# Turning the output projection's rows and the V values on VectorE in 32x32 squares instead of on TensorE

## The chip, the core and the metric

The kernel runs on one core of one Trainium2 chip. The metric is the time of one execution on the device in microseconds; of several runs the median counts. A core has five engines, each with an instruction stream of its own, which wait for each other by semaphores: TensorE (PE: matmuls; PEld is its weight loads), VectorE (DVE), ScalarE (ACT), GpSimd (POOL) and SyncE (SP), which here only issues DMA transfers. ScalarE issues some transfers too. An engine takes its stream in the order in which it is written, so an instruction that waits holds up those behind it.

## The reference: what is computed

One step of a two-layer streaming encoder, 2048 prompt rows and 32 sample rows of width 1024, in float32. Cut to the parts that the change touches:

```python
def delta_layer(x, ...):                       # layer A
    ...
    o, s_new = gated_delta_rule(q, k, v, g, beta, s0)
    o = o * lax.rsqrt(jnp.mean(o * o, -1, keepdims=True) + RMS_EPS) * norm_w * jax.nn.silu(z)
    out = o.reshape(b, l, A_VW) @ w_out        # output projection of layer A
    return layer_norm(DN_ALPHA * x + out, ln_g, ln_b), new_buf, s_new

def shared_kv(h, w_kv, pos):                   # h is layer A's result
    kv = h @ w_kv
    k = rope_partial(kv[..., :B_KVW]..., pos)
    v = kv[..., B_KVW:]...
    return k, v

def swa_layer(x, k, v, ...):                   # layer B
    proj = x @ w_in                            # queries and gates
    ...                                        # banded or cached attention on k, v
    return layer_norm(DN_ALPHA * x + (o * jax.nn.silu(z)) @ w_out, ln_g, ln_b)
```

`layer_norm` takes mean and variance of a row, and gives (x - mean) * rsqrt(var + eps) * g + b.

## The kernel before, in words

Float32 products are made of three matmuls each of high and low parts (`_hi`, `_lo`). The program has five stages: the projections and convolutions of layer A (to about 700 us), the delta rule (to about 1120 us), the output projection O1 of layer A (from 1080 to 1333 us, its first tiles woven into the delta rule's end), the projections P2 of layer B (from about 1310 to 1700 us, its first steps woven into O1's end) and the attention with the second output projection.

**O1** (classes `OutNorm` and `O1`) goes over 17 tiles of 128 rows, the last of 32. For each tile `g` (the gated result, with the channel on the partition) is loaded and split: ScalarE casts the high part `g_hi` (L1168), VectorE subtracts the low part `g_lo` (L1169). `r` (rows of x) is loaded (L1161). For each of two halves of 512 columns, TensorE makes 24 matmuls (L1126 to L1128) into a PSUM bank `po`, and VectorE empties the bank into `r` (L1134) and takes statistics (L1186). Then VectorE gets mean and inverse deviation by a chain of small instructions on a column (L1188 to L515), and normalizes `r` in four instructions of 512 columns (L1203, L1205). `r` is stored as `h` (L1265, to the memory `s_h`). `turned` is a generator: eight TensorE transposes of 128x128 in two groups of four (L1232), each group copied from PSUM to `hT` by ScalarE or VectorE (L1234), then one store of 512 KB to `s_hT` (L1236), in runs of 128 tokens (512 bytes). Its two groups are interleaved late in the matmuls of the next tile. `po` has two banks; the transposes take a third and fourth, which are two `po` banks for the first tiles and the `ps` banks of P2 once that exists.

**Order.** A scheduler sets the order on the engines, except where a block fixes TensorE's order, or more engines', as written: TensorE, VectorE and ScalarE during the delta rule; TensorE and VectorE in O1's rest; all engines in P2. SP issues the loads of `g` and `r` for tiles below about 10, then ScalarE does. `r`, `g_hi` and `g_lo` have two buffers each, `g` and `hT` have one.

**P2** goes over column blocks of 416 tokens. For the two tiles that hold V, `turn` turns the 128x416 block `c` (ten calls): four TensorE transposes of 128x104 into the one bank `tp` (L1714), two ScalarE copies of 104x256 into two `o` buffers (L1718), each with a store by ScalarE's queue to `s_bv` (L1719). The `o` buffers are shared with all other work of P2 (11 of them). The weights' low part `w_lo` is made by VectorE (L1330).

Of the kernel before, what the change touches and what calls it, by code (L numbers as in the profile page):

```python
# [1140 lines left out]
class OutNorm:  # L1141
# [21 lines left out]

    def split(self, g, n):
        nc = self.nc
        ghi = self.two.tile([128, KC, 128], F32R, tag="g_hi", name="g_hi")
        glo = self.two.tile([128, KC, 128], F32R, tag="g_lo", name="g_lo")
        nc.scalar.copy(ghi[:, :, :n], g[:, :, :n])  # L1168
        nc.vector.tensor_tensor(out=low_part(ghi, glo, n), in0=g[:, :, :n], in1=ghi[:, :, :n], op=ALU.subtract)  # L1169
        return ghi, glo  # L1170

    def tile(self, parts, r, n, tail=False):
# [5 lines left out]
        for c in range(2):  # L1178
            cs = slice(c * 512, c * 512 + 512)
            ps = self.pp.tile([128, 512], F32, tag="po", name="po")  # L1180
            for k in range(KC):
                out_products(nc, ps, ghi, glo, (w[0][:, k, cs], w[1][:, k, cs]), k, n)
                if k % 2 == 1:
                    yield (4 if n <= 64 else 6) * 0.227
            add_products(nc, r, glo, ps, cs, n)
            V.bn_stats(out=st[:n, c, :], in_=r[:n, cs])  # L1186
# [7 lines left out]
        if not tail:  # L1194
            nb = self.two.tile([128, 1], F32, tag="nb", name="nb")
            V.scalar_tensor_tensor(out=nb[:n], in0=mv[:n, 0:1], scalar=-1.0, in1=rs[:n], op0=ALU.mult, op1=ALU.mult)
            nc.scalar.activation(r[:n], r[:n], AF.Identity, bias=nb[:n, 0:1], scale=rs[:n, 0:1])
            nc.gpsimd.tensor_tensor(out=r[:n], in0=r[:n], in1=tabs[0][:n], op=ALU.mult)
            nc.gpsimd.tensor_tensor(out=r[:n], in0=r[:n], in1=tabs[1][:n], op=ALU.add)
        else:  # L1200
            for c in range(2):
                cs = slice(c * 512, c * 512 + 512)
                V.scalar_tensor_tensor(out=r[:n, cs], in0=r[:n, cs], scalar=mv[:n, 0:1], in1=tabs[0][:n, cs],  # L1203
                                       op0=ALU.subtract, op1=ALU.mult)
                V.scalar_tensor_tensor(out=r[:n, cs], in0=r[:n, cs], scalar=rs[:n, 0:1], in1=tabs[1][:n, cs],  # L1205
                                       op0=ALU.mult, op1=ALU.add)
# [3 lines left out]
class O1:  # L1210
    def __init__(self, tc, es, I, O, T, G):
        self.nc, self.I, self.T, self.G = tc.nc, I, T, G
        self.on = OutNorm(tc, es, "o1", "left", I, "a", 2, T["wo"])
        self.bank = lambda: self.on.pp.tile([128, 512], F32, tag="po", name="tr")
        self.steps = 0
        self.room = lambda: self.on.one.tile([128, KC, 128], F32, tag="g", name="hT")
# [7 lines left out]
    def turned(self, h, c0, row, n):  # L1224

        nc, T = self.nc, self.T
        hT = self.room()
        for q in range(2):
            tr = self.bank()[:].rearrange("p (j t) -> p j t", j=4)
            for j in range(4):  # L1230
                k = q * 4 + j
                nc.tensor.transpose(tr[:, j, :n], h[:n, k * 128:k * 128 + 128], self.G["ident"][:n, :n])  # L1232
            copy = nc.scalar.copy if n == 128 and (q == 0 or c0 == 0) else nc.vector.tensor_copy
            copy(hT[:, q * 4:q * 4 + 4, :n], tr[:, :, :n])  # L1234
            if q == 1:
                nc.sync.dma_start(T["hT"][:, :, c0:c0 + n].rearrange("h p t -> p h t"), hT[:, :, :n])  # L1236
            yield 0.44

    def tiles(self, tiles, ready, more):


        late = iter(())
# [5 lines left out]
        for i, t in enumerate(tiles):  # L1248
# [9 lines left out]
            for j, out in enumerate(self.on.tile(got, r, t[2], True)):  # L1258
                if isinstance(out, float):
                    yield out  # L1260
                    if j == 3 and ahead is not None:
                        ahead = self.on.split(ahead, tiles[i + 1][2])
                    if j >= 6:
                        yield from itertools.islice(late, 1)
            self.nc.sync.dma_start(self.T["h"][t[1]:t[1] + t[2], :], out[:t[2]])  # L1265
            late = self.turned(out, *t)
# [4 lines left out]
        yield from late  # L1271


class P2:
# [29 lines left out]
    def open_left(self, left):  # L1304
# [4 lines left out]
        self.py = new_pool(self.tc, left, "p2_py", 1, PSUM, side="left")  # L1309
# [400 lines left out]
    def turn(self, c, half, b):  # L1710
        nc, w = self.nc, TB // 4
        tp = self.py.tile([128, 4, 128], F32, tag="tp", name="tp")
        for j in range(4):
            nc.tensor.transpose(tp[:w, j, :], c[:, j * w:j * w + w], self.ident[:, :])  # L1714
        rows = self.T["bv"][b * TB:(b + 1) * TB, half * 128:half * 128 + 128].rearrange("(j t) x -> t j x", j=4)
        for js in (slice(0, 2), slice(2, 4)):
            v = self.out()[:, 0:256].rearrange("p (j x) -> p j x", j=2)
            nc.scalar.copy(v[:w], tp[:w, js])  # L1718
            nc.scalar.dma_start(rows[:, js], v[:w])  # L1719
# [519 lines left out]
def program(tc, I, O, T, G):  # L2239
# [75 lines left out]
    o1[0].room = lambda: hp.tile([128, KC, 128], F32, tag="hT", name="hT")  # L2315
    o1[0].bank = p2[0].ps
# [216 lines left out]
```

## Time and profile before

| What | Value |
|---|---|
| Time, median of 3 runs | 2101.48 us (2099.33 to 2110.56) |
| The profiled execution: time and span | 2110.58 us; span 2108.8 us |
| Busy: PE, DVE, ACT, POOL | 97%, 70%, 47%, 43% of the span |
| Granted TensorE clock, mean | 0.989 |
| 1150 to 1250 us (O1): PE, DVE, ACT busy | 100.00, 81.24, 18.23 us of 100 |
| 1400 to 1700 us (P2): PE, DVE, ACT busy | 293.78, 232.95, 139.92 us of 300 |
| DMA packets; bytes | 292763; 360.85 MB |

How to read it: a row of the timeline has start, duration, engine, line, operation, out<-in by the program's names, and in brackets the engine's idle time before and what ended it. `SPq` and `ACTq` are transfers that these engines issue. A row of a group ends with its busy time, the mean in ns of one instruction, and the idle time before them with what ended most of it. A TensorE row with x4 is a run of four matmuls, whose times overlap.

### The profile page before, as it was taken

Reading aid. Unit: us, or ns where it says so; the run is one execution under the profiler, and the core shown is the slowest. Engines: PE = TensorE matmul, PEld = TensorE weight load, DVE = VectorE, ACT = ScalarE, POOL = GpSimd, SP = SyncE. Lnnn points to the kernel's source line nnn. Section 1 sums busy time; section 2 is a strip of 40 time slices with the busy share of each in tenths; the row PEclk is TensorE's granted clock in tenths of the full one; section 3 lists DMA queues with packets and bytes.
Section 4 is the critical chain, followed back from the end, with each engine's and each line's share of the span. In section 5 each row is a group of like instructions: output and inputs, shape, how many; then the busy total and the mean of one; then the engine's idle time right before and its main releaser. Section 6 shows DMA issues by size and latency. Waiting matters only on the chain.

```text
span 2108.8 us, 37301 instructions
## 1 busy us (share of the span) xinstructions
PE 2048.6 (97%) x13694; PEld 1875.4 (89%) x13694; DVE 1468.9 (70%) x2587; ACT 989.0 (47%) x2465; POOL 911.0 (43%) x1248
## 2 busy tenths in 40 slices
PE   7999999999999999999999999999999999999998
PEld 5999999999999999999887887889989997777775
DVE  4476666675647678888887887768877755566565
ACT  4354444446532267777762211534644445455552
POOL 0322223212222177778752112157436515566666
PEclk9999999999999999999999999999999999999999
DMA  5132333236665545455766666778776659533421
GB/s 206 33 90 88 97 110 111 82 102 226 193 185 179 182 137 179 159 169 182 271 209 227 212 213 219 254 229 296 243 240 222 226 171 317 127 101 107 114 72 66
DMA packets 292763, 360.85 MB, mean 171 GB/s; under 512 B 74260, under 2 KB 217460, under 8 KB 292564
## 3 DMA queue, kind: packets, MB, share of 16 engines
q1 hardware_dynamic: 278576, 334.29, 49.9%
q10 hardware_dynamic: 14004, 24.17, 3.6%
q8 instruction: 108, 1.77, 0.3%
q14 instruction: 75, 0.61, 0.1%
HBM read 235.54 MB, written 134.06 MB: 175 GB/s over the span
## 4 chain that ended last, share of the span: by engine, by line
PE 83%; DMA 7%; DVE 3%; POOL 3%; issue 2%; ACT 1%; SPq 0%; ACTq 0%; DVEq 0%; POOLq 0%
PE ps L79 12%; PE ps L81 11%; PE ps L80 11%; PE ot L1126 3%; PE ot L1127 3%; PE ot L1128 3%; PE S L1992 2%; PE po L1126 2%; PE ot L2025 2%; PE po L1128 2%; PE po L1127 2%; PE tr L2007 2%; PE X L1653 2%; PE X L1651 2%; PE X L1652 2%
## 5 line engine op out<-in xcount | busy, mean ns | idle before, releaser
L79 PE MATMUL ps<-act_hi,w_hi 128*128 128x416 f32 x1280 | 454.9, 355 | 0.0
L81 PE MATMUL ps<-act_hi,w_lo 128*128 128x416 f32 x1280 | 450.2, 352 | 0.0
L80 PE MATMUL ps<-act_lo,w_hi 128*128 128x416 f32 x1280 | 447.9, 350 | 0.0
L79 PEld LDWEIGHTS ps<-act_hi,w_hi 128*128 128x128 f32 x1280 | 240.3, 188 | 3.8 <-issue 0.4
L80 PEld LDWEIGHTS ps<-act_lo,w_hi 128*128 128x128 f32 x1280 | 240.6, 188 | 3.0
L81 PEld LDWEIGHTS ps<-act_hi,w_lo 128*128 128x128 f32 x1280 | 240.1, 188 | 3.3
L209 DVE SCALAR_TENSOR_TENSOR y<-R,convw,y 128x2083 f32<-128x2083 f32 x72 | 182.5, 2536 | 60.9 <-ACT y L206 44.9
L56 POOL TENSOR_TENSOR w_lo<-w_raw,w_hi 128x1024 fp32r<-128x1024 f32 x25 | 71.4, 2858 | 330.9 <-ACT w_hi L55 303.6
L729 POOL TENSOR_TENSOR tm<-L,Tt 128x60 f32<-128x60 f32 (+19 forms) x365 | 132.5, 363 | 84.8 <-issue 39.9
L1826 POOL TENSOR_TENSOR P<-e,sm 128x384 f32<-128x384 f32 (+2 forms) x128 | 102.3, 820 | 118.0 <-DVE sm L1816 111.6
L731 POOL TENSOR_TENSOR Tt<-Tt,tm 128x60 f32<-128x60 f32 (+19 forms) x365 | 139.8, 383 | 28.6
L1812 ACT ACTIVATE e<-S,nm 128x193 f32<-128x193 f32 (+2 forms) x260 | 104.6, 415 | 97.3 <-DVE nm L1807 56.5
L1330 DVE TENSOR_TENSOR w_lo<-w_raw,w_hi 128x512 fp32r<-128x512 f32 x132 | 136.7, 1053 | 18.5 <-ACT w_hi L1342 12.7
L1126 PE MATMUL po<-wo_hi,g_hi 128*128 128x512 f32 x256 | 104.9, 410 | 8.1 <-DVE r L1134 7.9
L305 ACT COPY R<-ps 128x416 f32<-128x416 f32 (+1 forms) x144 | 60.4, 442 | 109.3 <-PE ps L81 95.8
L1482 ACT ACTIVATE o<-X 128x416 f32<-128x416 f32 x80 | 41.4, 518 | 134.7 <-PE X L1653 134.6
L1126 PE MATMUL ot<-wo,g_hi 128*128 128x512 f32 x256 | 103.6, 405 | 0.0
L1128 PE MATMUL po<-wo_hi,g_lo 128*128 128x512 f32 x256 | 101.2, 396 | 0.5 <-DVE g_lo L1169 0.5
L1127 PE MATMUL po<-wo_lo,g_hi 128*128 128x512 f32 x256 | 101.1, 395 | 0.0
L1127 PE MATMUL ot<-wo,g_hi 128*128 128x512 f32 x256 | 100.8, 394 | 0.0
L1128 PE MATMUL ot<-wo,g_lo 128*128 128x512 f32 x256 | 100.8, 394 | 0.0
L1342 ACT CAST w_hi<-w_raw 128x512 fp32r<-128x512 f32 x129 | 76.8, 616 | 21.5 <-PE ps L1652 6.7
(362 smaller groups left out, 5119.4 us busy)
## 6 DMA issues: line engine op xcount, KB each, us to landing
w_raw<-in_b_w SPq DMA_DIRECT2D x60, 512.0 KB
w_raw<-in_w_in SPq DMA_DIRECT2D x40, 512.0 KB
act_raw<-s_hT SPq DMA_DIRECT2D x64, 208.0 KB
s_rows<-o SPq DMA_DIRECT2D x50, 208.0 KB
k<-s_k SPq DMA_DIRECT2D x17, 512.0 KB
E<-s_E SPq DMA_DIRECT2D x17, 512.0 KB
s_bq<-s_rows SPq DMA_DIRECT2D x40, 208.0 KB
s_bz<-o SPq DMA_DIRECT2D x40, 208.0 KB
```

The lines of the kernel that those rows point to most:

```text
L79: nc.tensor.matmul(ps, hi[:, k, :], xh[:, k, :], start=(k == 0), stop=False)
L80: nc.tensor.matmul(ps, hi[:, k, :], xl[:, k, :], start=False, stop=False)
L81: nc.tensor.matmul(ps, lo[:, k, :], xh[:, k, :], start=False, stop=(k == KC - 1))
L209: nc.vector.scalar_tensor_tensor(out=y[:], in0=R[:, j:j + W], scalar=self.convw[:, i, j:j + 1], in1=y[:], op0=ALU.mult, op1=ALU.add)
L729: P.tensor_tensor(out=tm[:n, i0 - k:, :w], in0=L[:n, i0:, j:j + 1].to_broadcast(sh), in1=Tt[:n, j:j + 1, :w].to_broadcast(sh), op=ALU.mult)
L731: P.tensor_tensor(out=Tt[:n, i0:, :w], in0=Tt[:n, i0:, :w], in1=tm[:n, i0 - k:, :w], op=ALU.subtract)
L1126: nc.tensor.matmul(ps[:n], ghi[:, k, :n], hi, start=a, stop=False)
L1127: nc.tensor.matmul(ps[:n], ghi[:, k, :n], lo, start=False, stop=False)
L1128: nc.tensor.matmul(ps[:n], glo[:, k, :n], hi, start=False, stop=z)
L1330: P.tensor_tensor(out=lo, in0=raw, in1=hi, op=ALU.subtract)
L1812: self.nc.scalar.activation(x.e[:, h, u, :x.n], x.S[:, h, u, :], AF.Exp, bias=x.nm[:, h, u:u + 1], scale=1.0, accum_out=x.sm[:, h, u:u + 1])
L1826: self.nc.gpsimd.tensor_tensor(out=x.P[:, u, :nj * 128].rearrange("r (j h k) -> r j h k", h=2, k=64), in0=x.e[:, :, u, :n].rearrange("r h ...
```

## The change

The tile's rows are turned by one VectorE instruction, `transpose`, which turns each square of 32x32 in its place. The squares are put where they belong by the store: four transfers of 32 partitions each, in runs of 32 tokens (128 bytes). `turned` is no generator any more and runs at the tile's end. The normalization becomes one small VectorE instruction (`nb`), one ScalarE Identity with scale and bias over 128x1024, and two VectorE products with the tables over 128x1024. The second half of a tile takes its bank from P2's `ps` once P2 exists, so that with it there are four banks. In P2 V is turned in the same way into one `o` buffer, and four stores by ScalarE's queue follow one step later; the bank `tp` is gone, and that pool (`py`) has two.

```diff
+    spare = None
+    def bank(self, c):
+        if c and self.spare:
+            return self.spare()
+        return self.pp.tile([128, 512], F32, tag="po", name="po")
...
-            ps = self.pp.tile([128, 512], F32, tag="po", name="po")
+            ps = self.bank(c)
...
-            for c in range(2):
-                cs = slice(c * 512, c * 512 + 512)
-                V.scalar_tensor_tensor(out=r[:n, cs], in0=r[:n, cs], scalar=mv[:n, 0:1], in1=tabs[0][:n, cs],
-                                       op0=ALU.subtract, op1=ALU.mult)
-                V.scalar_tensor_tensor(out=r[:n, cs], in0=r[:n, cs], scalar=rs[:n, 0:1], in1=tabs[1][:n, cs],
-                                       op0=ALU.mult, op1=ALU.add)
+        nb = self.two.tile([128, 1], F32, tag="nb", name="nb")
+        V.tensor_scalar(out=nb[:n], in0=mv[:n, 0:1], scalar1=rs[:n, 0:1], scalar2=-1.0, op0=ALU.mult, op1=ALU.mult)
+        nc.scalar.activation(r[:n], r[:n], AF.Identity, bias=nb[:n, 0:1], scale=rs[:n, 0:1])
+        V.tensor_tensor(out=r[:n], in0=r[:n], in1=tabs[0][:n], op=ALU.mult)
+        V.tensor_tensor(out=r[:n], in0=r[:n], in1=tabs[1][:n], op=ALU.add)
...
         hT = self.room()
-        for q in range(2):
-            tr = self.bank()[:].rearrange("p (j t) -> p j t", j=4)
-            for j in range(4):
-                k = q * 4 + j
-                nc.tensor.transpose(tr[:, j, :n], h[:n, k * 128:k * 128 + 128], self.G["ident"][:n, :n])
-            copy = nc.scalar.copy if n == 128 and (q == 0 or c0 == 0) else nc.vector.tensor_copy
-            copy(hT[:, q * 4:q * 4 + 4, :n], tr[:, :, :n])
-            if q == 1:
-                nc.sync.dma_start(T["hT"][:, :, c0:c0 + n].rearrange("h p t -> p h t"), hT[:, :, :n])
-            yield 0.44
+        self.nc.vector.transpose(hT[:n], h[:n])
+        rows = self.T["hT"].rearrange("h (c j) t -> j (h c) t", j=32)
+        for a in range(0, n, 32):
+            self.nc.sync.dma_start(rows[:, :, c0 + a:c0 + a + 32],
+                                   hT[a:a + 32].rearrange("j (c i) -> j c i", i=32))
...
-        self.py = new_pool(self.tc, left, "p2_py", 1, PSUM, side="left")
+        self.py = new_pool(self.tc, left, "p2_py", 2, PSUM, side="left")
...
     def turn(self, c, half, b):
-        nc, w = self.nc, TB // 4
-        tp = self.py.tile([128, 4, 128], F32, tag="tp", name="tp")
-        for j in range(4):
-            nc.tensor.transpose(tp[:w, j, :], c[:, j * w:j * w + w], self.ident[:, :])
-        rows = self.T["bv"][b * TB:(b + 1) * TB, half * 128:half * 128 + 128].rearrange("(j t) x -> t j x", j=4)
-        for js in (slice(0, 2), slice(2, 4)):
-            v = self.out()[:, 0:256].rearrange("p (j x) -> p j x", j=2)
-            nc.scalar.copy(v[:w], tp[:w, js])
-            nc.scalar.dma_start(rows[:, js], v[:w])
+        nc, t = self.nc, self.out()
+        nc.vector.transpose(t[:], c[:])
+        rows = self.T["bv"][b * TB:(b + 1) * TB, half * 128:half * 128 + 128]
+        rows = rows.rearrange("(b i) (a j) -> a i b j", i=32, j=32)
+
+        def store():
+            for a in range(4):
+                s = slice(32 * a, 32 * a + 32)
+                nc.scalar.dma_start(rows[a], t[s].rearrange("i (b j) -> i b j", j=32))
+
+        self.delay(store, 1)
...
-    o1[0].bank = p2[0].ps
+    o1[0].on.spare = p2[0].ps
```

Where the order on the engines moves, it is shown before and after. First VectorE in a steady tile of O1, from the end of the column chain (L515) to the second half's statistics; before:

```order
L515 TENSOR_SCALAR ln_y<-ln_t,ln_y 128x1
L1203 SCALAR_TENSOR_TENSOR r<-r,mv,ln_g 128x512
L1205 SCALAR_TENSOR_TENSOR r<-r,ln_y,ln_b 128x512
L1203 SCALAR_TENSOR_TENSOR r<-r,mv,ln_g 128x512
L1205 SCALAR_TENSOR_TENSOR r<-r,ln_y,ln_b 128x512
L1169 TENSOR_TENSOR g_lo<-g,g_hi 128x1024
L1134 SCALAR_TENSOR_TENSOR r<-r,po 128x512
L1186 BN_STATS st<-r 128x6
L1234 COPY hT<-ps 128x512
L1134 SCALAR_TENSOR_TENSOR r<-r,po 128x512
L1186 BN_STATS st<-r 128x6
```

and after:

```order
L515 TENSOR_SCALAR ln_y<-ln_t,ln_y 128x1
L1202 TENSOR_SCALAR nb<-mv,ln_y 128x1
L1204 TENSOR_TENSOR r<-r,ln_g 128x1024
L1205 TENSOR_TENSOR r<-r,ln_b 128x1024
L1226 STREAM_TRANSPOSE hT<-r 128x1024
L1176 TENSOR_TENSOR g_lo<-g,g_hi 128x1024
L1134 SCALAR_TENSOR_TENSOR r<-r,po 128x512
L1193 BN_STATS st<-r 128x6
L1134 SCALAR_TENSOR_TENSOR r<-r,ps 128x512
L1193 BN_STATS st<-r 128x6
```

The four normalizing instructions became `nb`, two products and the turn, with ScalarE's Identity between `nb` and the first product; the copy of `hT` between the two halves is gone.

Next ScalarE at the end of the delta rule (L784 to L903 are the delta rule's, `vs` is what its next matmuls read); before:

```order
L784 COPY ta<-tp 64x256 x2
L794 COPY u<-up 64x8x64 x2
L803 COPY ta<-y2p 64x256 x2
L813 ACTIVATE u<-u2p 64x4x64 x2
L863 COPY vs<-vp_11841 128x512
L884 COPY o<-op_11807 128x512
L863 COPY vs<-vp_11885 128x512
L903 ACTIVATE vn,Xo<-o 128x128 x4
```

and after:

```order
L784 COPY ta<-tp 64x256 x2
L794 COPY u<-up 64x8x64 x2
L803 COPY ta<-y2p 64x256 x2
L813 ACTIVATE u<-u2p 64x4x64 x2
L1203 ACTIVATE r<-r,nb,ln_y 128x1024
L863 COPY vs<-vp_11841 128x512
L884 COPY o<-op_11807 128x512
L863 COPY vs<-vp_11892 128x512
L903 ACTIVATE vn,Xo<-o 128x128 x4
```

The Identity of tile 0 (L1203) stands ahead of the copy of `vs`.

Last SP's transfers around the loads of `g` for tiles 2 to 4 (L1156); `w_raw` are weights of P2, and `s_g<-z` stores the delta rule's results; before:

```order
L1236 DMA s_hT<-hT 128x8x128
L1336 DMA w_raw<-in_b_w 128x1024 x4
L679 DMA z<-s_z 128x4x32
L1156 DMA g<-s_g 128x1024
L1265 DMA s_h<-r 128x1024
L1336 DMA w_raw<-in_b_w 128x1024
L932 DMA s_g<-z 128x4x32
L932 DMA s_g<-z 128x512 x2
L1161 DMA r<-in_x 128x1024
L1156 DMA g<-s_g 128x1024
L1236 DMA s_hT<-hT 128x8x128
L1265 DMA s_h<-r 128x1024
```

and after:

```order
L679 DMA z<-s_z 128x4x32
L1325 DMA w_raw<-in_b_w 128x1024 x2
L932 DMA s_g<-z 128x4x32
L1255 DMA s_h<-r 128x1024
L1229 DMA s_hT<-hT 32x32x32 x4
L1161 DMA r<-in_x 128x1024
L932 DMA s_g<-z 128x512 x2
L1156 DMA g<-s_g 128x1024 x2
L1255 DMA s_h<-r 128x1024
L1229 DMA s_hT<-hT 32x32x32 x4
L1161 DMA r<-in_x 128x1024
L1156 DMA g<-s_g 128x1024
```

Before, a load of `g` stands between the weights' loads, ahead of the second store of `h`; after, two loads of `g` stand behind that store, its four `hT` stores and the load of `r`.

More of the change, by code (lines that the diff above doesn't have):

```diff
@@ L1170, in split, with tile @@
         return ghi, glo
-    def tile(self, parts, r, n, tail=False):
+    def tile(self, parts, r, n):
         nc, V = self.nc, self.nc.vector
@@ L1213, in __init__ @@
         self.on = OutNorm(tc, es, "o1", "left", I, "a", 2, T["wo"])
-        self.bank = lambda: self.on.pp.tile([128, 512], F32, tag="po", name="tr")
         self.steps = 0
-        self.room = lambda: self.on.one.tile([128, KC, 128], F32, tag="g", name="hT")
+        self.room = lambda: self.on.one.tile([128, D], F32, tag="g", name="hT")
     def fetch(self, c0, row, n):
@@ L1257, in tiles @@
             self.on.queue = self.nc.sync if i < 9 else self.nc.scalar
-            for j, out in enumerate(self.on.tile(got, r, t[2], True)):
+            for j, out in enumerate(self.on.tile(got, r, t[2])):
                 if isinstance(out, float):
@@ L1262, in tiles @@
                         ahead = self.on.split(ahead, tiles[i + 1][2])
-                    if j >= 6:
-                        yield from itertools.islice(late, 1)
             self.nc.sync.dma_start(self.T["h"][t[1]:t[1] + t[2], :], out[:t[2]])
-            late = self.turned(out, *t)
+            self.turned(out, *t)
             got, r = ahead, following
@@ L1270, in tiles @@
         yield from more(2)
-        yield from late
 class P2:
@@ L2314, in program @@
     hp = new_pool(tc, last, "o1_hT", 1, side="right")
[L2315 to L2316 removed]
+    o1[0].on.spare = p2[0].ps
+    o1[0].room = lambda: hp.tile([128, D], F32, tag="hT", name="hT")
     later = []
```

9 lines of the change are left out of this document (removed).

## The prediction

> **What bounds the kernel now.** I read the page first, its busy shares and the chain of waits.
>
> ```profile
> PE 2048.6 (97%) x13694; PEld 1875.4 (89%) x13694; DVE 1468.9 (70%) x2587; ACT 989.0 (47%) x2465; POOL 911.0 (43%) x1248
> PE 83%; DMA 7%; DVE 3%; POOL 3%; issue 2%; ACT 1%; SPq 0%; ACTq 0%; DVEq 0%; POOLq 0%
> ```
>
> TensorE is busy for 97% of the span and holds 83% of the chain, so work taken from it shortens the kernel wherever no other engine is just behind. That must be asked of two stages: the layer A output projection (O1, 1080 to 1333 us) and the pass over the V tiles (1340 to 1700 us). Next, TensorE's own waits between 1080 and 1720 us (engine, line, waited for: total, times, longest), and who held VectorE's L1134 up.
>
> ```profile
> PE po L1126 <- DVE r L1134: 7.9, 3, 3.8
> PE ps L1653 <- DVE w_lo L1330: 4.8, 2, 3.6
> PE tp L1714 <- ACT o L1718: 3.2, 2, 3.0
> PE sp L846 <- ACT vs L863: 1.2, 1, 1.2
>   DMA r<-in_x: 5.2, 2
> ```
>
> In O1 TensorE waits three times for VectorE to empty a bank (L1134), and two of those wait in turn for a load of `r`. In the V turns it waits for ScalarE's copies. Then one tile of O1 in the timeline, TensorE and VectorE.
>
> ```profile
> 1171.92 0.39 PE L1128 MATMUL po<-wo_hi,g_lo 128*128 128x512 f32 x1
> 1172.15 0.60 PE L1232 MATMUL ps<-ident,r 128*128 128x128 f32 x4
> 1172.51 0.48 PE L1126 MATMUL po<-wo_hi,g_hi 128*128 128x512 f32 x1
> ```
>
> ```profile
> 1172.79 0.69 DVE L1234 COPY hT<-ps 128x512 f32<-128x512 f32 x1 [1.91 <-PE ps L1232]
> 1173.40 0.68 DVE L1134 SCALAR_TENSOR_TENSOR r<-r,po 128x512 f32<-128x512 f32 x1
> 1177.26 0.74 DVE L1203 SCALAR_TENSOR_TENSOR r<-r,mv,ln_g 128x512 f32<-128x512 f32 x1
> 1180.16 1.22 DVE L1169 TENSOR_TENSOR g_lo<-g,g_hi 128x1024 fp32r<-128x1024 f32 x1
> 1181.30 0.68 DVE L1134 SCALAR_TENSOR_TENSOR r<-r,po 128x512 f32<-128x512 f32 x1
> 1182.02 0.69 DVE L1186 BATCH_NORM_STATS2 st<-r 128x6 f32<-128x512 f32 x1
> 1184.62 0.69 DVE L1234 COPY hT<-ps 128x512 f32<-128x512 f32 x1 [1.91 <-PE ps L1232]
> ```
>
> The period is 1184.62 - 1172.79 = 11.83 us. VectorE is idle for only 1.91 of it, waiting for TensorE. So TensorE bounds a steady tile, and VectorE is second with 9.92 us of work.
>
> **The change, part by part.** *TensorE's transposes in O1.* A group of four occupies 1172.15 to 1172.51, 0.36 us, and the next matmul is 0.48 instead of 0.39 us: 0.44 us a group. Two groups in each of 17 tiles are 34 groups, 15.0 us. A tile needs TensorE for 11.83 - 0.88 = 10.95 us afterwards.
>
> *VectorE's work per tile.* The copy of `hT` goes (1173.40 - 1172.79 = 0.61 us), as do the four L1203/L1205 (1180.16 - 1177.26 = 2.90). What stays is 9.92 - 0.61 - 2.90 = 6.41: the L1134-to-L1203 chain 3.86, g_lo 1.14, and L1134 with its statistics 1.41. What comes instead:
>
> ```profile
> L225 DVE STREAM_TRANSPOSE R<-th 128x2080 f32<-128x2080 f32 x16 | 37.5, 2341 | 37.8 <-ACT th L224 37.8
> L717 DVE STREAM_TRANSPOSE L<-nb 128x1024 f32<-128x1024 f32 x16 | 32.3, 2019 | 1.7 <-ACT nb L708 1.7
> L841 DVE TENSOR_TENSOR k<-k,gb 128x1024 f32<-128x1024 f32 x16 | 20.1, 1257 | 12.2 <-PE ktr L818 12.2
> L1881 ACT ACTIVATE r<-r,nb,ln_y 128x1024 f32<-128x1024 f32 x15 | 18.7, 1246 | 4.5 <-DVE nb L1877 4.5
> L1877 DVE TENSOR_SCALAR nb<-mv,ln_y 128x1 f32<-128x1 f32 x15 | 3.2, 215 | 0.5
> ```
>
> The new `nb` is 0.2 us (L1877). Then VectorE waits for ScalarE's Identity over 128x1024: 1.25 us (L1881) and about 0.1 of handing over. Behind that wait stand on VectorE both products with the tables, the turn, the next tile's g_lo and the L1134 that empties TensorE's bank. Each product is 1.14 (g_lo's slot, the same shape) to 1.26 us (L841). The turn over 1024 columns is 1.15 us by L225 (2341 x 1024/2080), or 2.02 by L717, whose input is a strided broadcast. `r` and `hT` are plain rows like L225's, so I take 1.15. Sum: 6.41 + 0.2 + 1.35 + 2 x 1.14 + 1.15 = 11.4 us; high end 6.41 + 0.2 + 1.35 + 2 x 1.26 + 2.02 = 12.5. So VectorE replaces TensorE as the bound of a steady tile: 11.4 against 10.95, a gain of 0.4 of the 0.88 us.
>
> The Trainium skill, VectorE: DVE Perf Modes, section "The three transpose paths", gives VectorE 311 ns for a 128x128 bf16 transpose of 32x32 blocks. By that figure eight such squares would be an estimated 2.5 us and the tile 12.8; no run here shows bf16, and L225 is against it with 144 ns a square.
>
> *The start of O1.* The order puts tile 0's Identity ahead of ScalarE's `vs` copy, where TensorE's delta rule waits (L846 above, already 1.2 us).
>
> ```profile
> 1112.24 0.59 ACT L863 COPY vs<-vp 128x512 f32<-128x512 f32 x1 [2.59 <-PE vp L846]
> 1115.25 0.21 DVE L515 TENSOR_SCALAR ln_y<-ln_t,ln_y 128x1 f32<-128x1 f32 x1
> 1137.54 0.53 SPq L1156 DMA_DIRECT2D g<-s_g  x1
> 1144.21 1.04 ACT L1168 CAST g_hi<-g 128x1024 fp32r<-128x1024 f32 x1 [10.17 <-DMA g<-s_g]
> ```
>
> The column `ln_y` is ready at 1115.46, so `vs` starts near 1115.46 + 0.2 + 1.25 = 1116.9 instead of 1112.24; of these 4.7 us about 1.6 lie beside other TensorE work: 3.1 us. On SP the load of g for tile 3 loses more. Before, it is issued at 1137.54 and cast 6.67 us later; now it stands behind s_h of tile 1, its four hT stores and a load of `r` that waits for that s_h to land, by my walk near 1147.7. Tile 3's first matmul, at 1147.26 before, then comes near 1155. This +7.7 contains the 3.1, and the wait of 2.9 us that was there.
>
> *Tiles 3 to 15.* The first and last of the 13 L1134:
>
> ```profile
> 1161.56 0.68 DVE L1134 SCALAR_TENSOR_TENSOR r<-r,po 128x512 f32<-128x512 f32 x1
> 1310.62 0.68 DVE L1134 SCALAR_TENSOR_TENSOR r<-r,po 128x512 f32<-128x512 f32 x1
> ```
>
> Twelve periods took 149.1 us, with two waits for `r` and a slow stretch after each long TensorE wait, as here:
>
> ```profile
> 1284.47 0.47 PE L1126 MATMUL po<-wo_hi,g_hi 128*128 128x512 f32 x1 [3.85 <-DVE r L1134]
> 1285.24 0.63 PE L1126 MATMUL po<-wo_hi,g_hi 128*128 128x512 f32 x1
> 1285.67 0.63 PE L1127 MATMUL po<-wo_lo,g_hi 128*128 128x512 f32 x1
> 1288.65 0.39 PE L1128 MATMUL po<-wo_hi,g_lo 128*128 128x512 f32 x1
> ```
>
> Eight matmuls went at 0.43 us instead of the 0.23 before and after: 1.6 us. Twelve at 11.4 are 136.8, so -12.3. One wait stays: from tile 11 the ScalarE queue has the load of `r`, which waits for an s_h store, ahead of the next Identity. I put it at 4.7 us, the two old waits for `r` (5.2) as its nearest row, and less than zero is excluded, because the load's place ahead of the Identity is new. The last tiles' transposes, with no VectorE work behind them, give -2. Four banks let TensorE run ahead but cannot raise VectorE's rate; I give them nothing beyond this. O1 in all: +7.7 - 12.3 + 4.7 - 2.0 = -1.9.
>
> *The V turns.* Ten groups of transposes go, with their copies.
>
> ```profile
> L1714 PE MATMUL tp<-ident,o 128*104 128x128 f32 x40 | 7.0, 303 | 3.2 <-ACT o L1718 3.2
> 1399.51 0.37 ACT L1718 COPY o<-tp 104x256 f32<-104x256 f32 x1 [4.40 <-DMA w_raw<-in_b_w]
> ```
>
> At 0.44 us a group they are 4.4 us. With them goes the wait of 3.2 us, which came from one bank and two `o` buffers per turn (the copy waited 4.40 for a buffer), and its slow stretch, 1.6 again. New on VectorE are ten transposes of 128x416, about 0.5 us each by L225, in a stage where TensorE already waits for its w_lo (4.8 us above): between 0 and 5 us, I take 1, since most of them fall into idle time. A new buffer wait would sit on VectorE's turn with w_lo behind it; one buffer instead of two makes it less likely. Sum: -4.4 - 3.2 - 1.6 + 1 = -8.2.
>
> *The stores.* Each tile's hT goes out in 4 x 1024 runs of 128 bytes instead of 1024 of 512. The page's queue row, and the queue with the small packets between 300 and 400 us:
>
> ```profile
> q1 hardware_dynamic: 278576, 334.29, 49.9%
> q10 hardware_dynamic: 581, 0.07, 0.4%
> ```
>
> On q10 581 packets of about 120 bytes took 0.4% of 16 x 100 us, 11 ns each; 4096 on 16 engines are 2.8 us a tile. The mean packet of q1 is 0.499 x 16 x 2108.8 / 278576 = 60 ns, which would be 15.4. I take 11, by size the nearest row: at that price the stores lie beside the tile's other work.
>
> **Sum.** -1.9 - 8.2 = -10.1 us. The profiled execution took 2110.6 us (span 2108.8 and 1.8 around it) and would come to 2100.5. It lies 9.1 us above the median of the runs shown, 2101.5, and the sum taken from that gives 2091 us, my forecast. It could be anywhere between 2081 and 2100 by the bounds of the first tiles' delay (3 to 13 us), the r wait (0 to 5) and the V turns.
>
> **Rivals.** *All of TensorE's time comes off* (VectorE at or below 10.95 a tile, g in time): -15 in O1, its waits 7.9 and their slow stretches 3, the V turns 8: about -34, 2068 us. For it: the two old r waits may vanish with another order. Against: the 1.35 us in which VectorE waits for ScalarE. Chance 0.17.
>
> *VectorE dearer.* It decides once the turn and both products pass 3.9 us together, where the tile passes the old 11.83. At 12.5, 15 tiles cost 16 us more than forecast: 2107. L717 speaks for it, L225 against. Chance 0.11.
>
> *The loads of O1 come late in every tile (slower).* SP's order before and after, by these rows:
>
> ```profile
> 1216.91 0.32 SPq L1156 DMA_DIRECT2D g<-s_g  x1
> 1220.89 0.37 SPq L1236 DMA_DIRECT2D s_hT<-hT  x1
> ```
>
> Before, g was issued 4 us ahead of the hT store; now both loads stand behind four stores (4 x 0.37 = 1.5 us) that wait for VectorE's turn. From that point a g has about 11.4 - 1.5 - 6.7 (its landing) - 1.2 (cast) = 2 us to spare. If loads land 4 us later, about 13 tiles lose 2 us each: +26, 2117 us. Against: the lag is covered by my numbers, narrowly. Chance 0.11.
>
> *The small stores are dear (slower).* At the 35 to 60 ns of larger packets the stores take 9 to 15 us of all engines in a tile of 11.4, loads wait, and O1 loses some 3 us a tile: +50, 2141 us. The Trainium skill, DMA: Bandwidth & Descriptors, Specifications, asks for 512 bytes or more for line rate and says that smaller writes are read, modified and written. By that rule this rival would decide; the 11 ns of q10 do not agree, though q10 was nearly empty. Chance 0.07.
>
> **How the numbers follow.** The forecast has 0.54, and about half of it lies below 2091. Half a per cent, 10.5 us, is about what a measurement of this kernel tells from no change, so faster means below 2091.0 and slower above 2112.0. Faster: 0.17 + 0.28 = 0.45. Slower: 0.11 + 0.07 + 0.03 of the dearer VectorE = 0.21. The same: 0.34. The range reaches from the full gain to just short of the late loads, 2068 to 2115.
>
> **What would show it.** L1126 waiting for DVE r L1134 in most tiles of O1, with a period near 11.4; ScalarE's L1203 under 1.3 us with VectorE idle before L1204; the turn L1226 near 1.15 us; a TensorE wait near 1145 to 1155 for g; no wait at L1714's place near 1400. I am wrong if the period is 10.95 (the first rival), if L1226 is near 2 us, if ScalarE's g_hi waits for g<-s_g in each tile, or if the DMA share of O1 goes to 0.9.

## The result, and the profile after

The changed kernel takes 2130.67 us (median of 4 runs, 2127.87 to 2136.08), the kernel before 2105.18 us in runs beside it (median of 4, 2099.33 to 2110.56). The ratio is 1.0125, with a 95% interval of 1.0103 to 1.0148: 25.5 us slower, where 10 us faster was forecast. The profiled execution of the changed kernel has a span of 2134.3 us, 25.5 more than the one of before.

The page shows that the work was taken off TensorE as meant, and that the time went into waiting.

```profile
PE 2034.5 (95%) x13518; PEld 1857.2 (87%) x13518; DVE 1478.4 (69%) x2580; ACT 993.9 (47%) x2445; POOL 901.7 (42%) x1248
```

TensorE is busy for 14 us less (2048.6 before) in a span that is 25.5 us longer, so it waits or sits idle some 40 us more. TensorE's waits between 1080 and 1740 us name the places.

```profile
PE po L1126 <- ACT g_hi L1175: 19.5, 1, 19.5
PE po L1128 <- DVE g_lo L1176: 12.9, 9, 3.7
PE X L1640 <- ACT o L1471: 12.0, 3, 4.8
PE vp L846 <- ACT vs L863: 4.1, 1, 4.1
```

To see where the time is lost, the two traces are cut at the same events: VectorE emptying the second half of tiles 0, 3, 10 and 16 of O1 (L1134), then the first and the last of the 80 ScalarE copies `o<-X` of P2. Times in us, worked out from the timelines:

| Stretch | Before | After | Difference |
|---|---|---|---|
| start to tile 0 | 1111.5 | 1108.3 | -3.2 |
| tile 0 to tile 3 | 50.0 | 70.7 | +20.6 |
| tile 3 to tile 10 | 82.8 | 82.6 | -0.2 |
| tile 10 to tile 16 | 79.0 | 81.8 | +2.8 |
| tile 16 to P2's first copy | 30.1 | 30.1 | 0.0 |
| P2's first to last copy | 367.2 | 370.8 | +3.6 |
| the rest | 388.1 | 389.9 | +1.8 |

The stretches ahead of tile 0 and after P2 vary by up to 9 and 5 us between the traces of all the kernels below, and the change adds no work there. The loss is the three tiles at the start of O1, and where a gain was forecast (O1's other tiles, P2) there is none.

**The start.** SP's timeline around the load of g for tile 3 (SPq is a transfer that SP issues, and the second column how long SP was at it):

```profile
1150.85 0.33 SPq L1255 DMA_DIRECT2D s_h<-r  x1
1152.13 2.83 SPq L1229 DMA_DIRECT2D s_hT<-hT  x4
1155.38 0.41 SPq L1161 DMA_DIRECT2D r<-in_x  x1
1157.77 0.32 SPq L1156 DMA_DIRECT2D g<-s_g  x1
```

The load is issued at 1157.77 instead of 1137.54, behind tile 1's store of `h`, its four hT stores, a load of `r` and two stores of the delta rule. Tile 1's store itself is late: it was issued at 1141.32 before. VectorE shows why, and what follows:

```profile
1131.72 0.68 DVE L1134 SCALAR_TENSOR_TENSOR r<-r,po 128x512 f32<-128x512 f32 x1
1141.19 0.29 DVE L929 TENSOR_TENSOR z<-otr,z 128x128 f32<-128x128 f32 x1 [7.87 <-DMA z<-s_z]
1141.40 0.68 DVE L1134 SCALAR_TENSOR_TENSOR r<-r,po 128x512 f32<-128x512 f32 x1
...
1164.88 1.23 DVE L1176 TENSOR_TENSOR g_lo<-g,g_hi 128x1024 fp32r<-128x1024 f32 x1 [11.60 <-ACT g_hi L1175]
```

Between the two halves of tile 1 stands an instruction of the delta rule's end (L929) that waits 7.87 us for a load. Before, tile 1's second half and its normalization stood ahead of that wait:

```profile
1131.73 0.69 DVE L1134 SCALAR_TENSOR_TENSOR r<-r,po 128x512 f32<-128x512 f32 x1 [1.22 <-PE po L1128]
1135.62 1.50 DVE L1203 SCALAR_TENSOR_TENSOR r<-r,mv,ln_g 128x512 f32<-128x512 f32 x1
1142.90 1.49 DVE L929 TENSOR_TENSOR z<-otr,z 128x128 f32<-128x128 f32 x3 [1.61 <-DMA z<-s_z]
```

After the change VectorE (at 1164.88) and TensorE then wait for g:

```profile
1164.90 0.80 PE L1126 MATMUL po<-wo_hi,g_hi 128*128 128x512 f32 x1 [19.52 <-ACT g_hi L1175]
```

Tile 3 starts at 1164.90 instead of 1147.26. Its first eight matmuls take 3.9 us and the next eight 1.8: the granted clock is 0.54 from 1165 to 1169 us and 1.00 in the ten us behind that.

**A steady tile.** VectorE in tile 2, from the end of its column chain to the next tile's second half:

```profile
1171.32 0.21 DVE L1202 TENSOR_SCALAR nb<-mv,ln_y 128x1 f32<-128x1 f32 x1
1172.85 1.22 DVE L1204 TENSOR_TENSOR r<-r,ln_g 128x1024 f32<-128x1024 f32 x1 [1.31 <-ACT r L1203]
1174.10 1.23 DVE L1205 TENSOR_TENSOR r<-r,ln_b 128x1024 f32<-128x1024 f32 x1
1175.36 1.25 DVE L1226 STREAM_TRANSPOSE hT<-r 128x1024 f32<-128x1024 f32 x1
1176.53 1.18 DVE L1176 TENSOR_TENSOR g_lo<-g,g_hi 128x1024 fp32r<-128x1024 f32 x1
1177.64 0.68 DVE L1134 SCALAR_TENSOR_TENSOR r<-r,po 128x512 f32<-128x512 f32 x1
1178.96 0.67 DVE L1134 SCALAR_TENSOR_TENSOR r<-r,ps 128x512 f32<-128x512 f32 x1
```

VectorE is never idle but for the 1.31 us in which ScalarE normalizes, and the next nb (1182.94) comes 11.62 us after this one: VectorE is the bound.

**Tiles 11 to 13.** A period of O1 is named here by the tile whose second half ends it. SP, ScalarE and VectorE in the period of tile 12, in which tile 11 is normalized and tile 10 stored:

```profile
1274.08 0.32 SPq L1255 DMA_DIRECT2D s_h<-r  x1
1276.18 7.53 SPq L1229 DMA_DIRECT2D s_hT<-hT  x4
...
1282.15 0.34 ACTq L1161 DMA_DIRECT2D r<-in_x  x1
1282.59 1.24 ACT L1203 ACTIVATE r<-r,nb,ln_y 128x1024 f32<-128x1024 f32 x1 [14.66 <-DMA g<-s_g]
...
1283.87 1.23 DVE L1204 TENSOR_TENSOR r<-r,ln_g 128x1024 f32<-128x1024 f32 x1 [4.81 <-ACT r L1203]
1287.74 1.25 DVE L1226 STREAM_TRANSPOSE hT<-r 128x1024 f32<-128x1024 f32 x1 [1.39 <-DMA s_hT<-hT]
```

The Identity stands behind ScalarE's load of `r` into the buffer of tile 10, which has to be turned and stored first; SP issues that store of `h` at 1274.08, behind loads and stores of P2. The four hT stores of tile 10 then keep SP for 7.53 us, and the turn of tile 11 waits for them. VectorE waits 4.81 us for the Identity here and 5.81 in the next period, against 1.31 in most others (1.58 and 2.18 in the two before).

**P2.** ScalarE at a V turn near 1605 us:

```profile
1605.63 6.79 ACTq L1709 DMA_DIRECT2D s_bv<-o  x4
1612.46 0.62 ACT L1331 CAST w_hi<-w_raw 128x512 fp32r<-128x512 f32 x1 [6.92 <-DMA s_bv<-o]
```

The four stores keep ScalarE for 6.79 us. Its waits over P2 (1330 to 1740 us) hold 27.7 us of this kind, of which there were none before:

```profile
ACT w_hi L1331 <- DMA s_bv<-o: 27.7, 7, 6.9
```

Behind them stand the casts and the copies `o<-X` for which TensorE waits (12.0 us above, 2.3 before; 4.8 of the 12.0 lie at 1388 us, ahead of the first of these stores). From 1605 to 1633 us, across the last four turns, the trace loses 6.1 us against the same steps before; from P2's first copy up to there it is 2.5 us shorter.

### The profile page after: what moved, and what is told of

Same layout as the page of the kernel before. It is cut to its first block, busy times and chain, and to the rows that moved or that the text cites. A ratio compares the mean times of both kernels' runs of the same rounds, so it can differ in the third digit from the quotient of the medians.

```text
span 2134.3 us, 36946 instructions
## 1 busy us (share of the span) xinstructions
PE 2034.5 (95%) x13518; PEld 1857.2 (87%) x13518; DVE 1478.4 (69%) x2580; ACT 993.9 (47%) x2445; POOL 901.7 (42%) x1248
## 5 line engine op out<-in xcount | busy, mean ns | idle before, releaser
L56 POOL TENSOR_TENSOR w_lo<-w_raw,w_hi 128x1024 fp32r<-128x1024 f32 x25 | 61.7, 2466 | 326.5 <-ACT w_hi L55 301.2
L1331 ACT CAST w_hi<-w_raw 128x512 fp32r<-128x512 f32 x129 | 77.2, 616 | 60.4 <-DMA s_bv<-o 27.7
L215 DVE SCALAR_TENSOR_TENSOR y<-th,y 128x2083 f32<-128x2083 f32 x24 | 55.9, 2328 | 37.6 <-ACT th L213 37.6
L1126 PE MATMUL po<-wo_hi,g_hi 128*128 128x512 f32 x144 | 60.7, 421 | 19.7 <-ACT g_hi L1175 19.7
L1361 POOL TENSOR_TENSOR act_raw<-act_raw 128x416 f32<-128x416 f32 x32 | 41.3, 1300 | 77.8 <-DMA act_raw<-s_hT 69.8
```

Of the source, the lines that this page charges most:

```text
L1126: nc.tensor.matmul(ps[:n], ghi[:, k, :n], hi, start=a, stop=False)
```

## The experiments

Each kernel is the changed one with the edit shown, unless said otherwise. Theory A, formed from the traces: the loss is made at a few places where the new order or the new stores make an engine wait, the start above all. Theory B, the rival: the stores in 128-byte runs burden the DMA, so that loads come late everywhere.

| | Edit | Median, us | Ratio to before, 95% interval |
|---|---|---|---|
| 1 | first two tiles as before | 2111.14 | 1.0033 [1.0019, 1.0046] |
| 2 | normalization as before | 2120.02 | 1.0066 [1.0042, 1.0090] |
| 3 | V turns as before | 2128.62 | 1.0110 [1.0082, 1.0138] |
| 4 | hT stored in 512-byte runs | 2129.51 | 1.0119 [1.0099, 1.0139] |
| 5 | 1 and 2 | 2105.84 | 0.9997 [0.9982, 1.0012] |
| 6 | 5, two hT buffers | 2102.52 | 0.9993 [0.9977, 1.0008] |
| 7 | 5, V stores by SP | 2100.80 | 0.9965 [0.9946, 0.9984] |
| 8 | 6, V turns as before | 2096.86 | 0.9961 [0.9946, 0.9976] |
| 9 | two yields in tile 1 | 2123.19 | 1.0085 [1.0071, 1.0099] |
| 10 | turns of tiles 0, 1 later | 2119.77 | 1.0076 [1.0055, 1.0096] |
| 11 | before, with the V turns only | 2107.02 | 1.0007 [0.9996, 1.0017] |
| 12 | 6 and 7 | 2094.38 | 0.9950 [0.9938, 0.9963] |

The kernel before had medians of 2104.82 beside 1 to 4, 2105.68 beside 5 to 8 and 2106.23 beside 9 to 12. The changed kernel had its own (2105.18), so a gain of 1 or 2 us against it says little.

**1. The first two tiles as before.** `turned_pe` is the old generator, with the old normalization.

```diff
-            self.turned(out, *t)
+            if i < 2:
+                late = self.turned_pe(out, *t)
+            else:
+                self.turned(out, *t)
```

> The changed kernel, but with the first two tiles of O1 normalized and turned as before (four VectorE instructions, TensorE transposes interleaved with the next tile). Theory A (the loss is made at a few places, the largest at the start: hT of tile 1 takes the only buffer of g, so the load of g for tile 3 waits for tile 1's stores, and VectorE waits for z ahead of tile 1's second half): TensorE's 19.5 us wait goes to 3 or 4, tile 3 begins near 1148 instead of 1164.9, and the time falls by 15 to 18 us, to about 2114. Theory B (the 128-byte stores burden the DMA everywhere, and the loads come late wherever there is a lot of traffic): the wait only moves, the time falls by less than 5 us.

It is 19.5 us faster than the changed kernel. From tile 0 to tile 3 its trace has 51.9 us, against 70.7 and, before, 50.0. The start alone is most of the loss; theory B had under 5 us. The edit puts several things back at once, which 9 and 10 take apart in part.

**2. The normalization as before.**

```diff
-        nb = self.two.tile([128, 1], F32, tag="nb", name="nb")
-        V.tensor_scalar(out=nb[:n], in0=mv[:n, 0:1], scalar1=rs[:n, 0:1], scalar2=-1.0, op0=ALU.mult, op1=ALU.mult)
-        nc.scalar.activation(r[:n], r[:n], AF.Identity, bias=nb[:n, 0:1], scale=rs[:n, 0:1])
-        V.tensor_tensor(out=r[:n], in0=r[:n], in1=tabs[0][:n], op=ALU.mult)
-        V.tensor_tensor(out=r[:n], in0=r[:n], in1=tabs[1][:n], op=ALU.add)
+        for c in range(2):
+            cs = slice(c * 512, c * 512 + 512)
+            V.scalar_tensor_tensor(out=r[:n, cs], in0=r[:n, cs], scalar=mv[:n, 0:1], in1=tabs[0][:n, cs],
+                                   op0=ALU.subtract, op1=ALU.mult)
+            V.scalar_tensor_tensor(out=r[:n, cs], in0=r[:n, cs], scalar=rs[:n, 0:1], in1=tabs[1][:n, cs],
+                                   op0=ALU.mult, op1=ALU.add)
```

> The changed kernel with the normalization as before (four VectorE instructions, no Identity on ScalarE). Theory A: VectorE needs 10.5 us a tile instead of 11.6, TensorE bounds steady tiles at 10.95, the waits of 4.8 and 5.8 us before L1204 go, and with the 4 us before the vs copy that is 10 to 16 us, to about 2118; the long wait at the start stays. Theory B: the period stays near 11.6 because loads come late; under 5 us.

10.7 us faster. Tiles 3 to 10 take 76.5 us instead of 82.6, most of them 10.47 or 10.88 us each: four VectorE instructions with 2.9 us are cheaper than nb, the wait for ScalarE and two products with 4.0 (1171.32 to 1175.36 above). Most of those tiles are even below the 10.95 that I gave TensorE. A new wait shows at tiles 12 and 13, of the turn for its one buffer:

```profile
1278.23 1.25 DVE L1227 STREAM_TRANSPOSE hT<-r 128x1024 f32<-128x1024 f32 x1 [3.53 <-DMA s_hT<-hT]
...
1294.40 1.25 DVE L1227 STREAM_TRANSPOSE hT<-r 128x1024 f32<-128x1024 f32 x1 [5.54 <-DMA s_hT<-hT]
```

With the Identity gone, the late stores of hT hold VectorE directly. The long wait at the start stays (17.05 us), as expected.

**3. The V turns as before** (the old `turn`, and `py` with one bank).

```diff
+            nc.tensor.transpose(tp[:w, j, :], c[:, j * w:j * w + w], self.ident[:, :])
...
+            nc.scalar.copy(v[:w], tp[:w, js])
+            nc.scalar.dma_start(rows[:, js], v[:w])
```

> The changed kernel with the V turns as before (TensorE transposes, ScalarE copies). Theory A: ScalarE is held for 2.2 to 6.8 us by each set of four V stores; between 1605 and 1630 this costs 7.7 us, the first six turns gained 4; so 3 to 5 us faster, about 2127. If instead the V turns gain what was forecast (8 us), this kernel is 8 us slower, about 2139. Theory B: the traffic of the V stores is small, within 2 us.

2 us faster by the medians, which the intervals do not separate from nothing; 8 us slower, as the forecast has it, is excluded. From P2's first to last copy its trace has 364.4 us, against 370.8; the part that is 2.5 us shorter with the new turns (up to 1605 us) is 2.3 us shorter here with the old ones, so that gain is not theirs.

**4. One store in 512-byte runs**, which leaves out the placing of the squares.

```diff
+            self.nc.sync.dma_start(self.T["hT"][:, :, c0:c0 + n].rearrange("h p t -> p h t"),
+                                   hT[:].rearrange("p (h t) -> p h t", t=n))
```

> The changed kernel with O1's hT of the 128-row tiles stored by one transfer in runs of 512 bytes; the squares are not placed, so values of layer A's rows land in wrong columns and layer B computes on them. Theory A: SP's issue falls from 2.8 to 0.4 us a tile, g for tile 3 comes 3 to 5 us earlier, the waits at tiles 11 to 13 shrink; 5 to 10 us faster, about 2123. Theory B: 15 us or more, most of the loss.

1 us faster, within the noise: theory B falls. The issue takes 0.37 us instead of 2.8 a tile, and in the trace the stretches from tile 0 to 3 and from tile 10 to 16 are 4.9 and 5.2 us shorter. But tiles 3 to 10 are 7.5 us longer, for the scheduler ordered ScalarE in another way:

```profile
1220.59 1.05 ACT L1175 CAST g_hi<-g 128x1024 fp32r<-128x1024 f32 x1 [11.62 <-DMA g<-s_g]
1221.55 1.24 ACT L1203 ACTIVATE r<-r,nb,ln_y 128x1024 f32<-128x1024 f32 x1
```

In these tiles the cast of `g_hi`, with its wait for a load, stands ahead of the Identity; in the changed kernel it stands behind it in all but the last. VectorE's waits for the Identity add up to 16.05 us from tile 3 to 10, against 9.44. With these 6.6 us given back the gain would be some 8 us, an estimate; that is what theory A has, and still short of theory B. The price of the small stores by themselves is not settled by it.

That the small runs do load the DMA shows between the second halves of tiles 3 and 10, in which both kernels move 16.59 MB on these two queues (queue: packets, MB, share of 16 engines); before, 1161.6 to 1244.4 us:

```profile
q1 hardware_dynamic: 11312, 15.55, 60.3%
q10 hardware_dynamic: 284, 1.04, 4.2%
```

and after, 1179.0 to 1261.6 us:

```profile
q1 hardware_dynamic: 33255, 16.07, 74.7%
q10 hardware_dynamic: 144, 0.52, 2.0%
```

The share goes from 64.5% to 76.7%. The difference is 0.122 x 16 x 82.7 = 161 us of an engine for 21,800 more packets, while the tiles took the same time (82.8 and 82.6).

**5. Both 1 and 2**, no other edit.

> The first two tiles turned as before, and the normalization as before in all tiles (the two kernels that gained most, together); the other tiles and V turned on VectorE. Theory A: the gains add: TensorE bounds steady tiles at 10.95 us, no wait of ScalarE in the tile; left are the waits of VectorE for the one hT buffer at tiles 12 and 13 (3.5 and 5.5 us in the second kernel) and the V stores; 2103 us, 8 below the first kernel. Rival: the turn itself and its stores cost what they save wherever they stand, so the two do not add, and it stays near 2111.

The gains add about as expected (2103 us): level with the kernel before. Tiles 3 to 10 take 78.1 us; tiles 12 and 13 still take 17.2 and 16.1.

**6. Two buffers for hT.**

```diff
-    hp = new_pool(tc, last, "o1_hT", 1, side="right")
+    hp = new_pool(tc, last, "o1_hT", 2, side="right")
```

> As the fifth kernel, with two buffers for hT in the tiles after the delta rule. Theory A: VectorE's waits for s_hT<-hT at tiles 12 and 13 (9 us of VectorE, about 7 of TensorE) go, unless the loads of r or g are late there too; 4 to 7 us faster than the fifth. Rival (the queue of SP, not the buffer, holds tiles 12 and 13): the wait moves to r<-in_x or g<-s_g with nearly the same length; under 2 us.

3.3 us below the fifth by the medians, while the two ratios to before overlap; unclear by the time. In the trace the turn no longer waits at tiles 12 and 13, and part of it came back as a wait for a load:

```profile
1261.64 0.69 DVE L1134 SCALAR_TENSOR_TENSOR r<-r,po 128x512 f32<-128x512 f32 x1 [2.15 <-DMA r<-in_x]
```

Tiles 10 to 16 take 74.6 us against 77.8 in the fifth.

**7. The V stores issued by SP.**

```diff
-                nc.scalar.dma_start(rows[a], t[s].rearrange("i (b j) -> i b j", j=32))
+                nc.sync.dma_start(rows[a], t[s].rearrange("i (b j) -> i b j", j=32))
```

> As the fifth kernel, with the four V stores of each turn issued by SP instead of ScalarE. Theory A (ScalarE is held while it issues): the waits X<-ACT o of TensorE near 1420 and 1620 go, P2 gains 6 to 8 us on the fifth kernel, about 2097; SP may pass part of it on to its loads. Rival (the V stores' traffic or the VectorE turns cause the P2 loss): no change, within 2 us.

5 us below the fifth by the medians, less than the 6 to 8 expected, with intervals that just overlap. P2 takes 365.0 us in its trace against 370.1 in the fifth's, with the VectorE turns and the traffic unchanged. ScalarE's wait of its weight casts for the stores (28.2 us in the fifth) is gone; one of 4.2 us is left, elsewhere:

```profile
ACT o L1493 <- DMA s_bv<-o: 4.2, 1, 4.2
```

**8. The sixth, with the V turns as before.** The edit is that of 3.

> As the sixth kernel (two hT buffers), with the V turns as before. Theory A: V on VectorE with ScalarE's stores is worth nothing or a loss of a few us, so this one is 1 to 4 us faster than the sixth, about 2097. Rival: without the V turns on VectorE it is 8 us slower than the sixth, as the forecast has it.

5.7 us below the sixth, more than expected; in the traces P2 is only 1.5 us shorter (367.3 against 368.8), so most of it is not located. With experiments 3 and 11 (2 and 0.8 us) this is the third comparison in which the new V turns with ScalarE's stores bring no gain.

**9. Two yields in tile 1.** They let the delta rule's steps run on for 0.88 us of TensorE's time, as the transposes did, and add no work.

```diff
+                    if j >= 6 and i == 1:
+                        yield 0.44
```

> The changed kernel with one edit: in tile 1 of O1 the two yields of 0.44 us, which the transposes used to give, are given again (no work with them), so that tile 1 ends after the delta rule as before. hT of tile 1 then has its own buffer, the load of g for tile 3 stands ahead of tile 1's stores on SP, and VectorE's wait for z behind tile 1's second half. Theory A: that is the whole start; the 19.5 us wait goes to 4 or less, 12 to 16 us faster than the changed kernel, about 2116 (ScalarE's Identity ahead of vs stays). Rival (the stores in small runs delay the loads at the start): under 5 us.

7.5 us, less than the 12 to 16 expected. The load of g for tile 3 is back in its place, 22.6 us after tile 0's second half (49.5 in the changed kernel, 26.0 before). The wait of 19.5 is gone with it, but another of 8.34 has come, since VectorE's turn of tile 1 now waits for memory that the delta rule's last stores still hold, with tile 3's g_lo behind it:

```profile
1149.61 1.25 DVE L1226 STREAM_TRANSPOSE hT<-r 128x1024 f32<-128x1024 f32 x1 [4.73 <-DMA s_g<-z]
```

**10. The turns of tiles 0 and 1 later**, behind the next tile's split of g, as the transposes were.

```diff
+                    if j == 6 and 0 < i <= 2:
+                        self.turned(*kept)
...
+            kept = (out, *t)
+            if i >= 2:
+                self.turned(*kept)
-            self.turned(out, *t)
```

> The changed kernel with the turn and stores of tiles 0 and 1 made in the next tile, behind its split of g: the loads of g for tiles 2 and 3 no longer wait for hT's stores in the same buffer as one would expect from tile 1, but VectorE's wait for z stays ahead of tile 1's second half. Theory A: about 10 of the 17.6 us at the start come from g behind the stores, 8 from the wait for z; this kernel gets 8 to 11 us, about 2121. If the wait for z alone makes the delay, it gains under 3; if the buffer alone, 15 or more.

10.9 us. VectorE still waits for z in tile 1 (8.83 us), and TensorE's wait for g is 9.57 instead of 19.52:

```profile
1146.64 0.29 DVE L929 TENSOR_TENSOR z<-otr,z 128x128 f32<-128x128 f32 x1 [8.83 <-DMA z<-s_z]
```

The load of g for tile 3 no longer stands behind tile 1's stores, but behind those of tile 0, which use its buffer as they did before the change. VectorE turns tile 0 only at 1146.85, right after the wait for z, and the load is issued at 1154.82, 39.9 us after tile 0's second half. So about half of the start is the load behind tile 1's normalization and stores; the rest goes through VectorE's wait for z, by this trace.

**11. The kernel before, with the V turns of the change alone.**

> The kernel before with the V turns of the change alone (VectorE, four stores by ScalarE). Theory A: ScalarE's hold gives back what TensorE saves: between 2 us faster and 4 us slower than before. The forecast had 8 us faster.

0.8 us slower, ratio 1.0007: no difference. Its ScalarE is held as in the changed kernel:

```profile
1576.73 6.44 ACTq L1720 DMA_DIRECT2D s_bv<-o  x4
1583.21 0.62 ACT L1342 CAST w_hi<-w_raw 128x512 fp32r<-128x512 f32 x1 [6.57 <-DMA s_bv<-o]
```

**12. The sixth and seventh together**: from tile 2 on rows turned by VectorE, old normalization, two hT buffers, V turned by VectorE and stored by SP.

> The seventh kernel (first two tiles turned as before, normalization as before, V stores by SP) with two buffers for hT. If the two gains add, 3 to 5 us below the seventh, about 2096 and below the kernel before by 9; if SP is the limit where O1's buffers and the V stores meet, no better than the seventh.

0.5% faster than the kernel before, and the fastest of all by its median. Tiles 3 to 10 take 76.6 us (82.8 before) and P2 363.4 (367.2); the start still costs 2.5 us more than before.

## Why the prediction was wrong, point by point

**TensorE's saving was right in the main.** It is busy for 14 us less, where 15.0 and 4.4 were forecast; the granted clock was lower, 0.984 instead of 0.989, but whether that is the 5 us between was not worked out. That it would not be had in full, since VectorE becomes the bound of a steady tile, was right too: 11.62 us a tile where no other wait falls, 11.4 forecast. The missing 0.2 is the two products, which took 1.25 us each where I took 1.14; the groups of VectorE show them and the turn:

```profile
L1205 DVE TENSOR_TENSOR r<-r,ln_b 128x1024 f32<-128x1024 f32 x16 | 20.5, 1284 | 0.6
L1204 DVE TENSOR_TENSOR r<-r,ln_g 128x1024 f32<-128x1024 f32 x16 | 20.4, 1275 | 31.1 <-ACT r L1203 31.1
L1226 DVE STREAM_TRANSPOSE hT<-r 128x1024 f32<-128x1024 f32 x16 | 19.9, 1245 | 1.9 <-DMA s_hT<-hT 1.4
```

The turn was 1245 ns long and took 1.17 us of VectorE's time, by L225's rate as taken. The estimate of 2.5 us from the Trainium skill (VectorE: DVE Perf Modes, "The three transpose paths") does not fit float32 rows here: 1245 ns are 156 ns for each 128x128 square, half of the 311 that it gives for bf16. With some tiles at 11.9 to 12.3, tiles 3 to 10 gained 0.2 us instead of the 3.0 that 0.43 a tile would have given. Experiment 2 shows what stood in the way: the new normalization, not the turn. It also shows that a tile needs TensorE for at most 10.47 us, not the 10.95 of the sum; whether the two more banks have a part in that was not tested.

**The steps that failed** are three terms of the sum, each by about 12 us:

| Term | Forecast, us | Measured, us |
|---|---|---|
| the start of O1 | +7.7 | +20.6 (tile 0 to tile 3) |
| tiles 3 to 16: -12.3 + 4.7 - 2.0 | -9.6 | +2.6 (-0.2 and +2.8) |
| the V turns | -8.2 | +3.6 in P2, +0.8 alone (experiment 11) |

**The start of O1.** In absolute times tile 3's first matmul came 17.6 us late (1164.90 against 1147.26); counted from tile 0, which came 3.2 us earlier in this trace, it is 20.8. The mechanism, the load of g behind tile 1's stores, was named; its size was not. My walk had the load issued near 1147.7, and it was issued at 1157.77. What I did not price is that L929 with its wait for z stands ahead of tile 1's second half, so tile 1's nb came at 1145.39 instead of the 1135.62 at which its old normalization started: 9.8 us, nearly all of the 10.1. I took the normalization and the stores of tile 1 at their old time; from there to the load the walk's 12.1 us were right (12.4). I also treated it as a matter of SP's order alone, while `room` gives hT of tile 1 the buffer of `g`, so that the load cannot start before tile 1's stores have landed, whatever the queue; SP waited 0.6 us for that here. Experiment 1 shows that these tiles are 19.5 us of the loss, experiment 9 that the wait for g goes when the load has its old place, and 9 and 10 that neither edit gives all of it back. The Identity ahead of `vs` cost 2.9 (a wait of 4.1 instead of 1.2), 3.1 forecast.

**Tiles 3 to 16.** The twelve periods that took 149.1 us took 151.6, where 12 x 11.4 + 4.7 = 141.5 were forecast. Of the 10.1 us between, 2.6 are the longer steady period (11.62), 1.3 three slower tiles before tile 10, and 6.2 the waits behind tile 10: they add 10.9 us to tiles 11 to 15, not 4.7. A wait for `r` ahead of the Identity from tile 11 on was forecast; VectorE's waits for the Identity in the periods of tiles 12 and 13 are 4.81 + 5.81 - 2 x 1.31 = 8.0 us longer than elsewhere. What I did not see is that the single hT buffer stands beside it: SP issues the stores late, behind the loads and sums of P2, and takes up to 7.5 us for four of them. I had given the four issues 4 x 0.37 = 1.5 us; they take 2.8 in a quiet stretch. TensorE's granted clock from tile 10 to 16 was 0.92, against 0.98 before: behind the wait that ends at 1306 us its matmuls come every 0.43 us, and every 0.23 at the full clock. The -2.0 of the last tiles did not come (12.81 us for the last period, 12.76 before).

**The V turns** were forecast at -8.2 and are worth nothing (experiment 11). TensorE's transposes went, and the wait L1714 <- o with them, but the forecast had no term for ScalarE issuing four stores in small runs, which keep it for 2.2 to 6.8 us a turn. TensorE's wait near 1400 came back at the same step under another name:

| | Before | After | 11 | 7 |
|---|---|---|---|---|
| TensorE's wait for ScalarE's `o` (copies and tp) in P2, us | 5.5 | 12.0 | 8.1 | 4.2 |
| first to last `o<-X` in P2, us | 367.2 | 370.8 | 369.5 | 365.0 |

With SP as the issuer (experiment 7) part of the forecast gain appears: 5 us below the fifth kernel.

**The rivals.** "All of TensorE's time comes off" falls with the period of 11.62 us, "VectorE dearer" with the turn and both products at 3.7 us, under the 3.9 at which it decides. "The loads of O1 come late in every tile" gave 2117 us and the right sign, but the loads of steady tiles were in time; one load, at the start, was 20 us late. "The small stores are dear" (+50 us) is not borne out: 512-byte runs gain 1 us, or some 8 by the estimate in experiment 4. The Trainium skill (DMA: Bandwidth & Descriptors, Specifications) puts line rate at 512 bytes and more; the trace agrees in so far as 28,672 packets of 128 bytes in seven tiles raised the queues' share from 64.5% to 76.7% for the same bytes. That is at least 5.6 ns each (161 us / 28,672), and more by what the 7,168 packets of 512 bytes took that they replaced; I had taken 11. The DMA had room for it: those tiles took the same time.

## What to carry to other kernels

When a step moves from "late in the next tile" to "at this tile's end", ask what it takes with it at once: its buffer, the stores that must land before the buffer is free, and the place of every other instruction that is interleaved by the work's length; a change that only takes work away can move those too. Price a store by how long the engine that issues it is held, not by its bytes alone, and give it to an engine behind which nothing urgent stands. Before taking an instruction count for a gain, sum the wait between engines with it: four VectorE instructions of 0.73 us beat two of 1.25 with a ScalarE step between.

## What the runs showed of the hardware

Issuing a transfer is not of constant length. Four hT stores of 32x32x32 took SP 2.8 us in quiet stretches and up to 7.5 at tile 12, where one store of the same bytes in 512-byte runs took 0.45 (experiment 4; 0.37 in quiet stretches); four V stores took ScalarE 2.2 to 6.8 us, the old pair 0.31 each. Whether it is the length of the runs, the number of transfers or what else is in the queue that sets this was not taken apart.
